# Sparse attention: the second parts of queries and keys stacked into the scores' contraction, the causal mask as a product, and two steps moved later

## The chip, the cores and the metric

The kernel runs on one core of a Trainium2 chip. The metric is the device time of one execution in microseconds; the median of the runs is compared, less is better. The core's engines run side by side, each through its own instructions in order: TensorE (PE in the profile; its weight loads, PEld, overlap its products), VectorE (DVE), ScalarE (ACT), GpSimd (POOL), and SyncE (SP), which here only issues transfers. TensorE writes its results to PSUM, eight banks of 512 fp32 values in each of 128 partitions.

## The reference

Two networks of two layers each run one after the other on 256 tokens of width 1024. Ten stages: feed-forward, S5, feed-forward, feed-forward, convolution, feed-forward, retention, PEER (experts), sparse attention (`nsa`), PEER. The change is in `nsa` alone. Cut to what matters (one batch, 256 tokens, 16 heads of 64 in 4 groups that share keys and values):

```python
kv = (xs @ w_kv)          # three branches, each with keys and values of 4 groups x 64
# branch 0, compressed: blocks of 32 tokens every 16, through a small MLP -> 15 keys and values
hid = gelu(einsum('cbgnf,cfh->cbgnh', blocks, cmp_w1) + cmp_b1); comp = einsum(..., hid, cmp_w2)
q = (h @ w_in)[..., :1024].reshape(...) * 64 ** -0.5;  gate = sigmoid((h @ w_in)[..., 1024:])
o_cmp = softmax(q @ k_cmp, blocks that have ended) @ v_cmp
o_slc = softmax(q @ k_slc, chosen blocks, causal)  @ v_slc
o_win = softmax(q @ k_win, last tokens, causal)    @ v_win
out = gate0 * o_cmp + gate1 * o_slc + gate2 * o_win;  return out @ w_o
```

With 256 tokens every block is chosen and the window covers all, so the second and third branch are plain causal attention over up to 256 keys, each with its own keys and values.

## The kernel before

Large matrix products run as three fp32r products each (`mm3`, lines L281 to L283): both factors are split into a first part (`h`, rounded by a ScalarE copy) and a second part (`l`, what is left, a VectorE subtraction), and hh, hl and lh are summed in PSUM. Weights come as 1 MB units (`wload`), and are split into `wh` (L264) and `wl` (L265). `lin_b` multiplies 256 features (two halves of 128) by all 256 tokens into one PSUM bank; its 48 products have 256 columns. `tile_T` transposes rows of x and writes the split, transposed input (`xTh`, `xTl`); `apply_pending` makes the rows of x themselves (the scale and shift of the layer norm that the stage before left open, L1244 and L1245, two row tiles in halves: eight VectorE operations), which only the residual sum at the end of `nsa` reads.

`nsa` runs in this order. The values `V`; the branch-0 keys and values into `kv2` (two copies of the tokens, the second shifted by one); the keys of branches 1 and 2 into `kT` (`lin_b` for each branch, L1441 and L1442 copy it out of PSUM): fp32, with partitions 0 to 63 holding a group's keys beside zeros and partitions 64 to 127 zeros beside the same keys, so that one product serves two heads that are stacked in the contraction of 128. Then `apply_pending`, the compression (32 input tiles `nsfl`, L1461, times `cmp_w1`, L1463), four query products (`query`, L1475: one ScalarE copy out of PSUM each), the gates.

The attention loop goes over 16 pairs of heads: 8 pairs for query tile 0 (128 queries, n = 128 keys), then 8 for query tile 1 (n = 256). `softmax(i)` computes a pair's scores and weights, `turn(i)` transposes the weights (L1587) and copies them out (half by ScalarE, L1594, half by VectorE, L1592), `attend(i)` multiplies them by the values (L1606). `softmax` runs two pairs ahead of `turn`. The compressed branch (`coarse_softmax`, `coarse_out`) stands in front of the loop and in its first passes; part of the output projection is issued near the end. The scores of a pair, before:

```python
for b in range(2):
    sp = self.mm()                                    # one of two PSUM buffers
    nc.tensor.matmul(sp[...], lhsT=qT[:, g, fb, tile], rhs=kT[:, b, g, :, :n], ...)      # L1565
    v.tensor_tensor(sm[:, b, :, :n], sp[...], mask[...], ALU.add)                        # L1568
v.tensor_reduce(nm, sm[:, :, :, :n], AX.X, ALU.max, negate=True)                         # L1571
for r in range(2):
    for b in range(2):
        nc.scalar.activation(sm[:, b, r, :n], sm[:, b, r, :n], AF.Exp, bias=nm..., accum_out=den...)  # L1574
```

PSUM tiles come from three sets: `acc` (4), `mm` (2) and `tr` (2); a set's next tile waits until the one in its place has been read. `hlp` holds one split transposed input (two tiles of 8 KB a partition), so each `new_T` waits for the last reader of the one before. The order within an engine is not the program's: a planner places each instruction, at build time, where its engine has nothing of higher rank ready, rank being the place in the program; an instruction can so run long before its neighbours. Copies by two engines out of one PSUM bank are put one behind the other at build time.

Of the kernel before, what the change touches and what calls it, by code (L numbers as in the profile page):

```python
# [10 lines left out]
F32 = mybir.dt.float32  # L11
F32R = mybir.dt.float32r
# [183 lines left out]
class Net:  # L196
# [1196 lines left out]
    def nsa(self):  # L1393
# [5 lines left out]
        with ExitStack() as cx:  # L1399
# [14 lines left out]
            mask, cmask = cload("ns_mask", [P, 2, S]), cload("ns_cmask", [P, 2, 2, 16])  # L1414
            pe, b1, w2 = cload("cmp_pe", [P, 2, 16]), cload("cmp_b1", [P, 2, 2]), cload("cmp_w2", [P, 2, 2, 64])
            wg = cload("ns_g", [P, NDC, 48], kp)

# [5 lines left out]
            kv2 = kp.tile([P, 2, 4, S], F32, name="ns_kv2")  # L1423
            for c in range(2):
                ps = self.mm()
                self.lin_b(xh, xl, self.I["ns_kc"][c], ps)
                for g in range(4):
                    q = slice(64 * (g % 2), 64 * (g % 2) + 64)
                    o = g // 2 * S
                    nc.scalar.activation(kv2[0:64, c, g, :], ps[q, o:o + S], AF.Copy)  # L1430
                    v.tensor_copy(kv2[64:128, c, g, 0:S - 1], ps[q, o + 1:o + S])
            kT = np_.tile([P, 2, 4, 2, S], F32, name="ns_kT")
            nc.gpsimd.memset(kT[0:64, :, :, 1, :], 0.0)
            nc.gpsimd.memset(kT[64:128, :, :, 0, :], 0.0)
            for b in range(2):
                ps = self.mm()
                self.lin_b(xh, xl, self.I["ns_k"][b], ps)
                for g in range(4):
                    q = slice(64 * (g % 2), 64 * (g % 2) + 64)
                    o = g // 2 * S  # L1440
                    nc.scalar.activation(kT[0:64, b, g, 0, :], ps[q, o:o + S], AF.Copy)  # L1441
                    v.tensor_copy(kT[64:128, b, g, 1, :], ps[q, o:o + S])  # L1442

            self.apply_pending()
# [4 lines left out]
            kcT = np_.tile([P, 4, 2, 16], F32, name="ns_kcT")  # L1449
            nc.gpsimd.memset(kcT, 0.0)  # L1450
# [3 lines left out]
            for c in range(2):  # L1454
                hp = [self.acc() for _ in range(2)]
                for u in range(2):
                    w1 = self.wload(self.I["cmp_w1"][c, u])
                    for j in range(8):
                        lc = u * 8 + j
                        fl = kp.tile([P, 4, 15], F32, tag="nsfl", bufs=4, name=self.nm("nsfl"))  # L1460
                        v.tensor_scalar(fl, kv2[:, c, :, 2 * lc:2 * lc + 225:16], pe[:, c, lc:lc + 1], None, ALU.add)  # L1461
# [3 lines left out]
                if c == 0:  # L1465
                    self.tile_T((hh, hl), src[1], 1, G, B)
# [3 lines left out]
            qT = np_.tile([P, 4, 2, S], F32, name="ns_qT")  # L1470

            def query(g):
                ps = self.mm()
                self.lin_b(hh, hl, self.I["ns_q"][g], ps)
                nc.scalar.activation(qT[:, g].rearrange("p f t -> p (f t)"), ps, AF.Copy, scale=0.125)  # L1475

            query(0)
            for c in range(2):
# [7 lines left out]
                if c == 0:  # L1486
                    for half in range(2):
                        nc.scalar.activation(kcT[64 * half:64 * half + 64, :, half, :15],
                                             cp[:64, :P].rearrange("p (g n) -> p g n", g=4)[:, :, :15], AF.Copy)
# [3 lines left out]
            query(1)  # L1493
            wgh, wgl = kp.tile([P, NDC, 48], F32R, name="ns_wgh"), kp.tile([P, NDC, 48], F32R, name="ns_wgl")
# [17 lines left out]
            def coarse_softmax(qt):  # L1512
                cs = self.tr()
                for p in range(8):
                    nc.tensor.matmul(cs[:, p * 32:p * 32 + 32], lhsT=qT[:, p // 2, p % 2, qt * P:qt * P + P],
                                     rhs=kcT[:, p // 2].rearrange("p r n -> p (r n)"), start=True, stop=True)
                sc = nw.tile([P, 16, 16], F32, tag="nssc", name=self.nm("nssc"))
                sh = [P, 16, 16]
                v.tensor_tensor(sc, cs[:, :S].rearrange("p (h n) -> p h n", h=16),
                                cmask[:, 0, qt, :].unsqueeze(1).to_broadcast(sh), ALU.add)  # L1520
# [35 lines left out]

            def softmax(i):
# [401 lines left out]
```

## Time and profile before

| | |
|---|---|
| median of 3 runs | 3199.25 us (3197.71 to 3201.43) |
| profiled execution | 3200.87 us, span 3199.1 us |
| mean granted TensorE clock | 0.989 |
| busy share: PE, PEld, DVE, ACT, POOL | 98%, 88%, 78%, 49%, 3% |
| sparse attention, first value product to last attend product | 2165.5 to 2322.4 us |

A busy share is a mean over stages with different limits; a cost in one stage is read from the stretch in which it lies. A profile row gives start, duration, engine, line and operation, out<-in, and behind it in brackets the idle time of the engine before it and what ended that. An fp32 product appears as two records, an fp32r product or a transpose as one. PE durations contain the pipeline's tail, so the price of one of many products is the distance from start to start.

### The profile page before, as it was taken

What the parts mean: (1) busy time and instruction counts of PE and PEld (TensorE: products, weight loads), DVE (VectorE), ACT (ScalarE), POOL (GpSimd) and SP (SyncE); (2) the same over time, 40 slices, a digit from 0 to 9 for tenths busy, and PEclk for the clock granted to TensorE, in tenths of its full rate; (3) what the DMA queues carried; (4) which work ended last, traced back from release to release, by engine and by line L of the source; (5) the groups of instructions that cost most, each with busy time, mean ns of one, the idle gap of its engine ahead of it and who ended that gap; (6) DMA issues with size and microseconds to landing.
All of it is one profiled execution on the core that took longest, in us unless ns stands there. A gap on an engine that the chain in (4) does not pass through costs nothing. (4 is left out here: it accounts for less than half of the span.)

```text
span 3199.1 us, 52281 instructions
## 1 busy us (share of the span) xinstructions
PE 3120.6 (98%) x20484; PEld 2829.5 (88%) x20484; DVE 2508.9 (78%) x4935; ACT 1567.3 (49%) x2350; POOL 105.0 (3%) x172
## 2 busy tenths in 40 slices
PE   8998999999999999999999999999999999999998
PEld 7888899898889888899999998888789999999887
DVE  8877867876986786899976666886789997666787
ACT  5556544446454443545654444335554665444432
POOL 1320000000000000000000000001000000000000
PEclk9999999999999999999999999999999999999999
DMA  5665767674266664445776666665044677566674
GB/s 212 209 230 184 290 228 278 242 287 146 89 242 244 251 250 169 168 153 200 231 255 214 215 215 212 228 226 194 32 159 160 206 235 258 201 215 215 211 239 163
DMA packets 174968, 668.36 MB, mean 209 GB/s; under 512 B 20705, under 2 KB 95233, under 8 KB 101762
## 3 DMA queue, kind: packets, MB, share of 16 engines
q1 hardware_dynamic: 150304, 606.05, 54.0%
q10 hardware_dynamic: 21826, 49.54, 4.1%
q0 software_dynamic: 2592, 9.44, 0.9%
q8 instruction: 161, 2.64, 0.3%
q14 instruction: 85, 0.70, 0.1%
HBM read 619.88 MB, written 45.11 MB: 208 GB/s over the span
## 5 line engine op out<-in xcount | busy, mean ns | idle before, releaser
L264 ACT ACTIVATE wh<-raw 128x1024 fp32r<-128x1024 f32 x948 | 998.5, 1059 | 1199.0 <-PE mm L282 617.6
L265 DVE TENSOR_TENSOR wl<-raw,wh 128x1024 fp32r<-128x1024 f32 x948 | 1150.1, 1221 | 403.9 <-ACT wh L264 392.9
L281 PE MATMUL mm<-xTh,wh 128*128 128x256 f32 x4032 | 1152.5, 286 | 4.5 <-ACT pg L1835 1.7
L283 PE MATMUL mm<-xTh,wl 128*128 128x256 f32 x4032 | 1142.5, 284 | 2.7 <-DVE wl L265 2.7
L282 PE MATMUL mm<-xTl,wh 128*128 128x256 f32 x4032 | 1144.5, 284 | 0.3 <-DVE xTl L355 0.3
L281 PEld LDWEIGHTS mm<-xTh,wh 128*128 128x128 f32 x4032 | 773.5, 192 | 15.7 <-ACT pg L1835 3.2
L282 PEld LDWEIGHTS mm<-xTl,wh 128*128 128x128 f32 x4032 | 773.6, 192 | 8.0 <-issue 0.7
L283 PEld LDWEIGHTS mm<-xTh,wl 128*128 128x128 f32 x4032 | 773.1, 192 | 4.7 <-DVE wl L265 4.4
L283 PE MATMUL acc<-wh,pal 128*128 128x512 f32 x1024 | 403.8, 394 | 0.0
L282 PE MATMUL acc<-wl,pah 128*128 128x512 f32 x1024 | 403.4, 394 | 0.0
L281 PE MATMUL acc<-wh,pah 128*128 128x512 f32 x1024 | 402.9, 393 | 0.0
L283 PEld LDWEIGHTS acc<-wh,pal 128*128 128x128 f32 x1024 | 192.6, 188 | 44.3
L281 PEld LDWEIGHTS acc<-wh,pah 128*128 128x128 f32 x1024 | 193.6, 189 | 39.3
L282 PEld LDWEIGHTS acc<-wl,pah 128*128 128x128 f32 x1024 | 192.7, 188 | 40.1
L1788 ACT ACTIVATE pwb<-tr 128x512 f32<-128x512 f32 x128 | 130.8, 1088 | 24.5 <-PE tr L1785 20.6
L281 PE MATMUL acc<-wh,gh 128*128 128x512 f32 x352 | 141.3, 402 | 0.0
L282 PE MATMUL acc<-wl,gh 128*128 128x512 f32 x352 | 139.8, 397 | 0.0
L283 PE MATMUL acc<-wh,gl 128*128 128x512 f32 x352 | 138.5, 399 | 0.3 <-DVE gl L405 0.3
L1781 DVE TENSOR_SCALAR poh<-pe_iota,pi,pwT 128x128 f32<-128x128 f32 x512 | 136.7, 338 | 0.0
L1849 DVE CAST pah<-pa 128x256 fp32r<-128x256 f32 x256 | 74.7, 293 | 69.6 <-PE acc L282 69.6
L1850 DVE TENSOR_TENSOR pal<-pa,pah 128x256 fp32r<-128x256 f32 x256 | 108.3, 424 | 25.3 <-DVE pah L1849 0.9
L1785 PE MATMUL tr<-poh,poh 128*128 128x128 f32 x1024 | 125.2, 275 | 1.6 <-ACT pwb L1788 1.6
(480 smaller groups left out, 3517.7 us busy)
## 6 DMA issues: line engine op xcount, KB each, us to landing
raw<-in_w SPq DMA_DIRECT2D x132, 1024.0 KB, 4.9
raw<-in_pe_u SPq DMA_DIRECT2D x128, 1024.0 KB, 4.8
raw<-in_pe_v SPq DMA_DIRECT2D x128, 1024.0 KB, 4.8
adaraw<-in_ada_w SPq DMA_DIRECT2D x48, 1024.0 KB, 6.9
pe_wscr<-pwb ACTq DMA_DIRECT2D x32, 1024.0 KB, 8.5
pwr<-pe_wscr SPq DMA_DIRECT2D x30, 1024.0 KB, 6.9
raw<-in_ret_vg SPq DMA_DIRECT2D x16, 1024.0 KB, 4.8
raw<-in_pe_wq SPq DMA_DIRECT2D x16, 1024.0 KB, 4.8
```

What stands on the lines that cost most here:

```text
L264: nc.scalar.activation(h, raw[:, sl], AF.Copy)
L265: nc.vector.tensor_sub(l, raw[:, sl], h.bitcast(F32))
L281: mm(out, lhsT=ah, rhs=bh, start=start, stop=False)
L282: mm(out, lhsT=ah, rhs=bl, start=False, stop=False)
L283: mm(out, lhsT=al, rhs=bh, start=False, stop=stop)
L1781: v.tensor_scalar(oh1[:, j, :], iota[:, :NK], i1[:, t:t + 1], wT[:, t:t + 1], ALU.is_equal, ALU.mult)
L1785: nc.tensor.matmul(ps[:, j * P:j * P + P], lhsT=oh2[:, t4 * 4 + j, :], rhs=oh1[:, t4 * 4 + j, :], start=True, stop=True)
L1788: nc.scalar.activation(wb[:, :, o:o + 4].rearrange("p i t -> p t i"), ps.rearrange("p (t i) -> p t i", t=4), AF.Copy)
L1849: v.tensor_copy(ah, a)
L1850: v.tensor_sub(al, a, ah.bitcast(F32))
```

## The change

Scores: the query tile keeps first parts and second parts of one head stacked in the contraction (64 + 64), and the keys' first parts and second parts lie in two tiles, `kT[0]` and `kT[1]`, each twice (both halves of the partitions). A product with `kT[0]` gives (qh + ql)·kh, one with `kT[1]` (qh + ql)·kl, both fp32r. One PSUM buffer now holds one head and both branches. The causal mask is added by a product of the identity (`one`) with the mask (`low`, twice side by side) over the last 128 keys of each branch. Maximum and exponentials read PSUM; there is no mask add and no copy of the scores in SBUF. The coarse scores take stacked queries too, 16 products of 32 columns per query tile, and one more add.

Order and storage: of the keys' second parts those of branch 1 are made at once, those of branch 2 after the compression's sums of its first half; `apply_pending` moves from ahead of the compression to behind `query(1)`; `softmax(0)` is written ahead of `coarse_softmax(0)`. `kv2` lies in the attention's output tiles, two of the three weight buffers in `hlp`.

```diff
-            mask, cmask = cload("ns_mask", [P, 2, S]), cload("ns_cmask", [P, 2, 2, 16])
+            cmask = cload("ns_cmask", [P, 2, 2, 16])
+            mask = np_.tile([P, P], F32, name="ns_mask")
+            nc.scalar.dma_start(out=mask, in_=self.I["ns_mask"][:, 0, :P])
...
-            kv2 = kp.tile([P, 2, 4, S], F32, name="ns_kv2")
+            kv2 = [o.rearrange("p h d -> p (h d)").rearrange("p (g t) -> p g t", g=4) for o in o_sb]
...
-            kT = np_.tile([P, 2, 4, 2, S], F32, name="ns_kT")
-            nc.gpsimd.memset(kT[0:64, :, :, 1, :], 0.0)
-            nc.gpsimd.memset(kT[64:128, :, :, 0, :], 0.0)
+            halves = [slice(0, 64), slice(64, 128)]
+            kT = [np_.tile([P, 4, 2, S], F32R, name="ns_kT" + i) for i in "hl"]
+            rest = []
+
+            def key_rest():
+                for three in sum(rest, []):
+                    v.tensor_sub(*three)
+                rest.clear()
+
             for b in range(2):
                 ps = self.mm()
                 self.lin_b(xh, xl, self.I["ns_k"][b], ps)
-                for g in range(4):
-                    q = slice(64 * (g % 2), 64 * (g % 2) + 64)
-                    o = g // 2 * S
-                    nc.scalar.activation(kT[0:64, b, g, 0, :], ps[q, o:o + S], AF.Copy)
-                    v.tensor_copy(kT[64:128, b, g, 1, :], ps[q, o:o + S])
-
-            self.apply_pending()
+                for r, q in enumerate(halves):
+                    src_, (h, l) = ps[q].rearrange("p (f t) -> p f t", f=2), (t[:, r::2, b, :] for t in kT)
+                    for d in (q, halves[1 - r]):
+                        nc.scalar.activation(h[d], src_, AF.Copy)
+                    rest.append([(l[d], src_, h[q].bitcast(F32)) for d in (q, halves[1 - r])])
+                if b == 0:
+                    key_rest()
+
+            one = np_.tile([P, P], F32R, name="ns_one")
+            nc.scalar.activation(one, self.ident, AF.Copy)
+            low = np_.tile([P, 2, P], F32R, name="ns_low")
+            for b in range(2):
+                nc.scalar.activation(low[:, b, :], mask, AF.Copy)
+
...
                 if c == 0:
+                    key_rest()
                     self.tile_T((hh, hl), src[1], 1, G, B)
...
-            qT = np_.tile([P, 4, 2, S], F32, name="ns_qT")
+            qT = np_.tile([P, 4, 2, 2, S], F32R, name="ns_qT")
...
-                nc.scalar.activation(qT[:, g].rearrange("p f t -> p (f t)"), ps, AF.Copy, scale=0.125)
+                for r, q in enumerate(halves):
+                    h, l = (qT[d, g, r].rearrange("p f t -> p (f t)") for d in (q, halves[1 - r]))
+                    nc.scalar.activation(h, ps[q], AF.Copy, scale=0.125)
+                    v.scalar_tensor_tensor(l, ps[q], 0.125, h.bitcast(F32), ALU.mult, ALU.subtract)
...
             query(1)
+            self.apply_pending()
...
-                for p in range(8):
-                    nc.tensor.matmul(cs[:, p * 32:p * 32 + 32], lhsT=qT[:, p // 2, p % 2, qt * P:qt * P + P],
-                                     rhs=kcT[:, p // 2].rearrange("p r n -> p (r n)"), start=True, stop=True)
+                for h in range(16):
+                    nc.tensor.matmul(cs[:, h * 32:h * 32 + 32], lhsT=qT[:, h // 4, h % 2, h % 4 // 2, qt * P:qt * P + P],
+                                     rhs=kcT[:, h // 4].rearrange("p i n -> p (i n)"), start=True, stop=True)
...
+            rooms = [t.bitcast(F32).rearrange("p d t -> p (d t)")[:, :4 * S] for t in self.new_T()]
+            rooms.append(nw.tile([P, 4 * S], F32, tag="nssm", bufs=1, name=self.nm("nssm")))
+            rooms = [t.rearrange("p (b r k) -> p b r k", b=2, r=2) for t in rooms]
...
-                sm = nw.tile([P, 2, 2, S], F32, tag="nssm", bufs=3, name=self.nm("nssm"))
-                for b in range(2):
-                    sp = self.mm()
-                    nc.tensor.matmul(sp[:, :2 * n].rearrange("p (r k) -> p r k", r=2),
-                                     lhsT=qT[:, g, fb, qt * P:qt * P + P],
-                                     rhs=kT[:, b, g, :, :n], start=True, stop=True)
-                    v.tensor_tensor(sm[:, b, :, :n], sp[:, :2 * n].rearrange("p (r k) -> p r k", r=2),
-                                    mask[:, qt, :n].unsqueeze(1).to_broadcast([P, 2, n]), ALU.add)
+                sm = rooms[i % 3]
                 nm = nw.tile([P, 2, 2], F32, tag="nsnm", bufs=3, name=self.nm("nsnm"))
-                v.tensor_reduce(nm, sm[:, :, :, :n], AX.X, ALU.max, negate=True)
                 for r in range(2):
+                    sp = self.mm()[:, :2 * n].rearrange("p (b k) -> p b k", b=2)
+                    q = qT[:, g, r, fb, qt * P:qt * P + P]
+                    nc.tensor.matmul(sp, lhsT=q, rhs=kT[0][:, g, :, :n], start=True, stop=False)
+                    nc.tensor.matmul(sp[:, :, n - P:], lhsT=one, rhs=low, start=False, stop=False)
+                    nc.tensor.matmul(sp, lhsT=q, rhs=kT[1][:, g, :, :n], start=False, stop=True)
+                    v.tensor_reduce(nm[:, r, :], sp, AX.X, ALU.max, negate=True)
                     for b in range(2):
-                        nc.scalar.activation(sm[:, b, r, :n], sm[:, b, r, :n], AF.Exp, bias=nm[:, b, r:r + 1],
+                        nc.scalar.activation(sm[:, b, r, :n], sp[:, b, :], AF.Exp, bias=nm[:, r, b:b + 1],
                                              accum_out=den[:, qt, 1 + b, h + r:h + r + 1])
...
+            softmax(0)
             coarse_softmax(0)
-            softmax(0)
             softmax(1)
```

## Rows read from the trace of the kernel before

**Rows 1.** The page's first part: busy us (share of span) and instructions by engine.
```profile
PE 3120.6 (98%) x20484; PEld 2829.5 (88%) x20484; DVE 2508.9 (78%) x4935; ACT 1567.3 (49%) x2350; POOL 105.0 (3%) x172
```

**Rows 2.** Windows: stretch, length, busy us (x instructions) by engine, PEclk, DMA share, GB/s.
```profile
2165.50:2181.10 15.60, 14.92 (x63) 11.62 (x64) 11.89 (x26) 6.34 (x13) 6.12 (x8) 0.89 0.42 130
2181.10:2222.00 40.90, 40.41 (x341) 39.55 (x340) 26.48 (x65) 18.37 (x40) 0.00 (x0) 1.00 0.49 181
2222.00:2247.90 25.90, 25.90 (x218) 25.71 (x216) 13.54 (x13) 15.69 (x21) 0.00 (x0) 1.00 0.67 244
2247.90:2258.10 10.20, 8.45 (x55) 6.81 (x53) 7.71 (x20) 5.97 (x20) 0.00 (x0) 1.00 0.28 104
2258.10:2280.90 22.80, 21.40 (x135) 17.38 (x135) 20.53 (x46) 14.81 (x62) 0.00 (x0) 1.00 0.00 1
2280.90:2322.40 41.50, 40.09 (x260) 31.66 (x259) 31.72 (x50) 21.93 (x74) 0.00 (x0) 1.00 0.00 1
```

**Rows 3.** Timeline of PE in the loop: start, us, line and operation.
```profile
2263.17 1.03 PE L1565 MATMUL mm<-ns_kT,ns_qT 128*128 128x256 f32 x4
2264.03 0.55 PE L1606 MATMUL acc<-ns_V,nspT 128*128 128x64 f32 x4
2264.43 0.39 PE L1587 MATMUL tr<-c_ident,nssm 128*128 128x128 f32 x2
...
2276.66 1.02 PE L1565 MATMUL mm<-ns_kT,ns_qT 128*128 128x512 f32 x2
2277.52 0.27 PE L1587 MATMUL tr<-c_ident,nssm 128*128 128x128 f32 x1
```

**Rows 4.** Groups by line and form, 2281 to 2323 us: busy us, mean ns | idle before.
```profile
L1574 ACT ACTIVATE nssm<-nssm,nsnm 128x256 f32<-128x256 f32 x31 | 15.3, 496 | 1.1 <-DVE nsnm L1571 1.0
...
L1568 DVE TENSOR_TENSOR nssm<-mm,ns_ns_mask 128x512 f32<-128x512 f32 x14 | 9.4, 683 | 1.6 <-PE mm L1565 1.5
L1571 DVE TENSOR_REDUCE nsnm<-nssm 128x4 f32<-128x1024 f32 x7 | 8.4, 1203 | 0.1
...
L1594 ACT ACTIVATE nspT<-tr 128x512 f32<-128x512 f32 x8 | 4.8, 597 | 9.9 <-PE tr L1587 9.7
```

**Rows 5.** The same, 2249 to 2281 us.
```profile
L1574 ACT ACTIVATE nssm<-nssm,nsnm 128x128 f32<-128x128 f32 x32 | 12.4, 389 | 4.9 <-DVE nsnm L1571 4.9
...
L1568 DVE TENSOR_TENSOR nssm<-mm,ns_ns_mask 128x256 f32<-128x256 f32 x16 | 6.4, 414 | 1.5 <-PE mm L1565 1.3
...
L1571 DVE TENSOR_REDUCE nsnm<-nssm 128x4 f32<-128x512 f32 x8 | 5.4, 678 | 0.1
```

**Rows 6.** Waits of PE's weight loads, 2247.9 to 2258.2 us: total, times, longest.
```profile
PEld mm L1565 <- DVE nssm L1568: 2.4, 3, 1.3
```

**Rows 7.** Timeline of PE at the last query and the first coarse scores.
```profile
2246.92 0.28 PE L281 MATMUL mm<-xTh,wh 128*128 128x256 f32 x1
...
2247.04 0.28 PE L282 MATMUL mm<-xTl,wh 128*128 128x256 f32 x1
...
2248.00 1.42 PE L1515 MATMUL tr<-ns_kcT,ns_qT 128*128 128x32 f32 x12
```

**Rows 8.** Timeline of PE in the output projection.
```profile
2316.09 0.39 PE L281 MATMUL acc<-wh,oTh 128*128 128x512 f32 x1
2316.32 0.40 PE L282 MATMUL acc<-wl,oTh 128*128 128x512 f32 x1
```

**Rows 9.** Groups by line and form, 2182 to 2222 us.
```profile
L1463 PEld LDWEIGHTS acc<-nsfl,raw 128*128 128x128 f32 x128 | 14.7, 192 | 0.7 <-DVE nsfl L1461 0.7
...
L1442 DVE COPY ns_kT<-mm 64x256 f32<-64x256 f32 x8 | 3.4, 423 | 3.8 <-ACT ns_kT L1441 3.7
...
L1441 ACT ACTIVATE ns_kT<-mm 64x256 f32<-64x256 f32 x8 | 3.0, 377 | 6.9 <-PE mm L283 4.9 <-DVE ns_kT L1442 1.9
```

**Rows 10.** Timeline of DVE as the stage begins.
```profile
2168.61 0.69 DVE L1244 TENSOR_TENSOR x<-z,rowbc 128x512 f32<-128x512 f32 x1 [1.07 <-DMA rowbc<-in_ln_r]
...
2177.94 0.55 DVE L1496 TENSOR_TENSOR ns_wgl<-ns_ns_g,ns_wgh 128x384 fp32r<-128x384 f32 x1
```

More of the change, by code (lines that the diff above doesn't have):

```diff
@@ L1429, in nsa @@
                     o = g // 2 * S
-                    nc.scalar.activation(kv2[0:64, c, g, :], ps[q, o:o + S], AF.Copy)
-                    v.tensor_copy(kv2[64:128, c, g, 0:S - 1], ps[q, o + 1:o + S])
-            kT = np_.tile([P, 2, 4, 2, S], F32, name="ns_kT")
-            nc.gpsimd.memset(kT[0:64, :, :, 1, :], 0.0)
-            nc.gpsimd.memset(kT[64:128, :, :, 0, :], 0.0)
+                    nc.scalar.activation(kv2[c][0:64, g, :], ps[q, o:o + S], AF.Copy)
+                    v.tensor_copy(kv2[c][64:128, g, 0:S - 1], ps[q, o + 1:o + S])
+            halves = [slice(0, 64), slice(64, 128)]
[5 more added lines that the diff above has]
+                rest.clear()
             for b in range(2):
@@ L1448, in nsa @@
             nc.gpsimd.memset(hid, 0.0)
-            kcT = np_.tile([P, 4, 2, 16], F32, name="ns_kcT")
-            nc.gpsimd.memset(kcT, 0.0)
+            kcT = np_.tile([P, 4, 2, 16], F32R, name="ns_kcT")
+            nc.gpsimd.memset(kcT.bitcast(F32), 0.0)
             vc = np_.tile([P, 4, 64], F32, name="ns_vc")
@@ L1460, in nsa @@
                         fl = kp.tile([P, 4, 15], F32, tag="nsfl", bufs=4, name=self.nm("nsfl"))
-                        v.tensor_scalar(fl, kv2[:, c, :, 2 * lc:2 * lc + 225:16], pe[:, c, lc:lc + 1], None, ALU.add)
+                        v.tensor_scalar(fl, kv2[c][:, :, 2 * lc:2 * lc + 225:16], pe[:, c, lc:lc + 1], None, ALU.add)
                         for hb in range(2):
@@ L1486, in nsa @@
                 if c == 0:
-                    for half in range(2):
-                        nc.scalar.activation(kcT[64 * half:64 * half + 64, :, half, :15],
-                                             cp[:64, :P].rearrange("p (g n) -> p g n", g=4)[:, :, :15], AF.Copy)
+                    cpv = cp[:64, :P].rearrange("p (g n) -> p g n", g=4)[:, :, :15]
+                    for q in halves:
+                        nc.scalar.activation(kcT[q, :, 0, :15], cpv, AF.Copy)
+                    for q in halves:
+                        v.tensor_sub(kcT[q, :, 1, :15], cpv, kcT[:64, :, 0, :15].bitcast(F32))
                 else:
@@ L1513, in coarse_softmax @@
                 cs = self.tr()
-                for p in range(8):
-                    nc.tensor.matmul(cs[:, p * 32:p * 32 + 32], lhsT=qT[:, p // 2, p % 2, qt * P:qt * P + P],
-                                     rhs=kcT[:, p // 2].rearrange("p r n -> p (r n)"), start=True, stop=True)
+                for h in range(16):
+                    nc.tensor.matmul(cs[:, h * 32:h * 32 + 32], lhsT=qT[:, h // 4, h % 2, h % 4 // 2, qt * P:qt * P + P],
+                                     rhs=kcT[:, h // 4].rearrange("p i n -> p (i n)"), start=True, stop=True)
+                cs = cs.rearrange("p (h i n) -> p h i n", h=16, i=2)
                 sc = nw.tile([P, 16, 16], F32, tag="nssc", name=self.nm("nssc"))
                 sh = [P, 16, 16]
-                v.tensor_tensor(sc, cs[:, :S].rearrange("p (h n) -> p h n", h=16),
-                                cmask[:, 0, qt, :].unsqueeze(1).to_broadcast(sh), ALU.add)
+                v.tensor_tensor(sc, cs[:, :, 0, :], cmask[:, 0, qt, :].unsqueeze(1).to_broadcast(sh), ALU.add)
+                v.tensor_add(sc, sc, cs[:, :, 1, :])
                 mx = nw.tile([P, 16], F32, tag="nscm", name=self.nm("nscm"))
```

## The prediction

> **What bounds the kernel now.** I read the page first, for the engine that is never free: TensorE is busy for 98% of the span [rows 1], so what counts is what the change takes from TensorE's queue or adds to it, and the waits in it. Then I cut the attention stage into stretches [rows 2]. From 2181.1 to 2247.9 (values, keys, compression, queries) TensorE is busy all but half a microsecond, while VectorE is busy 26.5 of 40.9 us and then 13.5 of 25.9, and ScalarE 18.4 and 15.7: work added to those two here has room. From 2247.9 the scores begin. Length less PE busy time gives TensorE's idle time there: 1.75 us in the opening, 1.40 in the loop's first half (query tile 0), 1.41 in its second half (query tile 1), 4.6 in all. VectorE is busy 20.5 of 22.8 us in the first half: the one stretch in which it is nearly the bound too. Last I read the rows of one pair [rows 3 to 5], for the price of each operation, and the waits of the opening [rows 6].
>
> **The scores' products.** A pair of heads needs two fp32 products before; each stands in the trace as two records. With 2n = 256 columns, four records take from 2263.17 to 2264.03, 0.86 us a pair; with 512 columns two take 2276.66 to 2277.52, so four take 1.72 [rows 3]. After, each head of the pair takes a product with the keys' first parts, one of 256 columns with the mask, and one with the second parts, all fp32r. The trace has that type in the projections: 512 columns follow each other by 0.23 us (2316.09 to 2316.32), 256 columns by 0.12 (2246.92 to 2247.04) [rows 7, 8]. Query tile 1: 2 × (0.23 + 0.12 + 0.23) = 1.16 us, 0.56 less, × 8 pairs = **-4.5**. Query tile 0: 6 × 0.12 = 0.72, 0.14 less, × 8 = **-1.1**.
>
> **The coarse scores.** Before 8 fp32 products of 32 columns for each query tile, two records each; 12 records take 1.42 us, 0.12 each [rows 7]. After there are 16 fp32r products of 32 columns. No row has that type so narrow. Upper bound 0.12, the price of 256 columns; lower bound 0.06, half of it, though nothing in these rows goes below 0.1. I take 0.12, since 32 and 256 columns cost the same in these rows: 32 × 0.12 against 32 × 0.12, **0**, bounds -1.9 and 0. VectorE gets one more add per tile, 0.41, beside idle time.
>
> **VectorE and ScalarE in the loop.** The mask adds go: 16 of 0.41 and 16 of 0.68 [rows 4, 5], 17.4 us of VectorE. The maximum, one reduce of 0.68 (1.20 for 1024 elements) from SBUF, becomes two from PSUM. No row has a reduce that reads PSUM; the add that reads PSUM takes 0.683 for 512 elements and the reduce from SBUF 0.678 [rows 4, 5], so I take 0.41 for 256 elements and 0.68 for 512: +0.14 and +0.16 a pair, +2.4 us in all. VectorE falls by 15 us of the 52 that it is busy in the loop. The exponentials keep their number and size and read PSUM; ScalarE's copies out of PSUM take 0.60 for 512 elements, the exponential from SBUF 0.50 for 256 [rows 4], so I leave 0.49 from one start to the next, 0.39 for 128 columns [rows 5].
>
> **What the buffers do.** A score buffer ("mm", two of them) was free once the mask add had read it. Now it is held until two exponentials have. Query tile 1: first head 0.58 for products, 0.27 to VectorE, 0.68, 0.05, 0.98 of exponentials: 2.56 us after the pair began. The second head's exponentials queue behind on ScalarE and end at 3.54; its buffer is wanted 0.58 into the next pair, so a period of 3.06 will do, or 3.66 with ScalarE's 0.60 copy of transposed weights between. TensorE's own period is 1.16 + 24 records (8 transposes, 16 for the values) of 0.10 [rows 3] = 3.6: the buffer is hidden, if barely. Query tile 0: 0.36 + 0.27 + 0.41 + 0.05 + 0.77 = 1.86, second head 2.63, period 2.63 + 0.1 - 0.36 = 2.37, or 2.8 with the copy of half the width (0.4, an estimate from the 0.60); TensorE's own is 0.72 + 12 × 0.10 = 1.9. Here the buffer is late, unless other products (coarse, transposes of a pair ahead, of which three buffers of weights allow two) fill in.
>
> **The waits in the loop.** In the opening TensorE's weight loads wait 2.4 us for the mask add [rows 6]; that wait has no instruction left to wait for. In its place: the last query is split by two copies and two subtractions, which take turns as the keys' copies do in the trace, 2 × (0.60 + 0.68) = 2.6 us where one copy of that width took 0.60 [rows 4]. Score 1 needs the buffer that this frees, and coarse heads 12 to 15 need its result. What can be issued meanwhile: coarse heads 0 to 11 (1.4) and score 0 (0.36). So 0.8 us idle, then about as much for the exponentials of pair 0: I take **-1.0**, between -1.75 (none left) and +1.5 (nothing fills in). In the first half, 1.40 idle with VectorE 90% busy; it loses about a third of its work, so its waits go, against the late buffer, up to 7 × 0.45 = 3.2. I take **-0.9**, between -1.4 and +3.2. In the second half **0**, down to -1.4.
>
> **Keys, queries, rows of x.** Keys: eight copies of 0.38 on ScalarE and eight of 0.42 on VectorE [rows 9] become eight of 0.60 and eight of 0.68, +1.8 and +2.1 us. Of the eight subtractions four follow their product at once, four stand behind the compression's first sums. VectorE is idle 14 us of that stretch; what is late if the cover fails is the compression's input tiles, for which TensorE's loads already wait 0.7 us [rows 9]. Cost 0, bounds -0.7 and +1.5. Queries: one copy each becomes two copies and two subtractions: ScalarE +2.4 us over four queries, VectorE +5.4; with their 15.7 and 13.5 of 25.9 us both stay under 20. Cost 0 while TensorE is supplied. ScalarE also makes one identity and two mask copies, and POOL's two fills of the key tile go; neither holds anything here. The mask's load is a quarter of its size on the same queue: 0.
>
> The eight operations on the rows of x come later in the program. In the trace they do not stand where the program has them: they fill VectorE's idle moments from 2168.61 on, and the subtraction for the gate weights, written much later still, comes right behind them at 2177.94 [rows 10]. So the engine order takes whatever is ready, and I expect these eight at the same place: **0**. Were they to leave, the first one's wait of 1.07 us for its DMA would leave the queue with them, and the normalisation queued behind it would come earlier: at best the 0.68 us that TensorE idles in that stretch [rows 2] plus some of its 1.07, -1.0 to -1.5. Were they to land among the queries, VectorE would have 13.5 + 5.4 + 5.4 = 24.3 of 25.9 us.
>
> **The sum.** -4.5 - 1.1 - 1.0 - 0.9 = -7.5 us. The profiled execution took 3200.87 us around a span of 3199.1; it becomes 3193.4. That execution is 1.6 above the median of 3199.25; against the median, 3191.75. Behind the attention TensorE is the bound again [rows 1], so what is won there is kept.
>
> **The rivals.** *The buffers eat half.* The late buffer in the first half costs its whole 3.2 us and no other wait there goes: -5.6 + 3.2 - 1.0 = -3.4, 3195.85. For: two buffers, one queue for all exponentials. Against: 1.2 of TensorE's 1.9 us in such a pair are not scores and can be issued meanwhile.
>
> *Slower: both buffers wait for the whole pair.* If the engine order puts a pair's four exponentials and the copy of transposed weights in front of the next pair's first product, the period is a chain: query tile 1, 1.16 + 0.27 + 0.68 + 4 × 0.49 + 0.6 + 0.15 = 4.8 against some 4.3 now (41.5 less some 7 for the projection's 24 products of 0.23 and 12 transposes, over 8); query tile 0, 0.72 + 0.27 + 0.41 + 4 × 0.39 + 0.4 + 0.15 = 3.5 against some 2.3 (0.86 + 1.2, and the idle 1.40 over 7 pairs). That is +4 and +9.6, less the 1.0 of the opening and some 3 that other products fill: +10, 3209. It decides from where the chain passes 3.6 and 1.9 us, TensorE's own periods. Against it: pairs run two ahead, and today ScalarE stands idle at the end of each pair. The Trainium skill ("VectorE: DVE Perf Modes", Rules for kernel authors) would lean this way: work on a matmul's output should first be copied to SBUF if many operations follow. The kernel before does that, with the mask add as the copy; the change reads PSUM three times instead. By that rule the time would be this rival's; no row here has such a reader, and the rows' price of a PSUM operand shows no surcharge [rows 4, 5].
>
> *The rows of x do leave the start:* -7.5 - 1.2, 3190.6. *They, or the subtractions, crowd the queries:* VectorE nearly full, TensorE short by some 2.5 us, 3194.25; the change then does half of what it says.
>
> **Chances.** Faster or slower is beyond 6.4 us, 0.2%, about what a measurement of this kernel can tell. The forecast 0.52 (its own range 3189 to 3194, so 0.43 of it beyond 6.4 us and 0.09 within), rows of x leave 0.12 (faster), buffers eat half 0.20 and crowded queries 0.04 (within), whole-pair chain 0.12 (slower). Faster 0.55, within 0.33, slower 0.12. Range 3187 to 3201: it holds all but the chain and a small rest below, where the narrow coarse products cost half and all waits go.
>
> **What would show it.** Right: no VectorE adds between score and maximum; score records at 0.23 and 0.12; the stretch from the last query's product to the last attend product 74.5 us before, 67 after; VectorE well under 80% there; the eight operations on x still in 2168 to 2178. Wrong: score loads that wait for exponentials for more than 3 us in all (buffers), a first half as long as before, or TensorE gaps between 2182 and 2248. A fall of the granted clock in the stage, now 1.00 from 2181 to 2322 [rows 2], would also break the sum.

## The result and the profile after

The changed kernel takes 3215.32 us (median of 6, 3211.72 to 3217.05), the kernel before 3198.48 beside it (median of 6, 3195.2 to 3201.43): a ratio of 1.0051, 95% interval 1.004 to 1.0062. The forecast was 3191.75. The profiled span is 3212.8 us, 13.7 more than before. (The medians lie 16.8 apart: the profiled execution of the kernel before was 2.4 above its median, that of the changed kernel 0.7 below.)

The page's first part, as in [rows 1]: all engines do about what they did.

```profile
PE 3130.8 (97%) x20516; PEld 2846.2 (89%) x20516; DVE 2504.5 (78%) x4931; ACT 1570.3 (49%) x2357; POOL 101.2 (3%) x170
```

Windows of the stage, columns as in [rows 2]: compression and queries, opening, rest of query tile 0, query tile 1.

```profile
2206.00:2259.50 53.50, 51.21 (x356) 50.31 (x355) 31.06 (x61) 25.73 (x42) 0.00 (x0) 0.81 0.47 177
2259.50:2270.00 10.50, 7.95 (x39) 6.61 (x38) 8.09 (x16) 7.65 (x26) 0.00 (x0) 0.66 0.29 101
2270.00:2293.50 23.50, 22.74 (x150) 20.40 (x148) 14.67 (x40) 11.40 (x51) 0.00 (x0) 0.86 0.00 1
2293.50:2336.00 42.50, 40.41 (x292) 36.26 (x291) 25.99 (x46) 22.56 (x81) 0.00 (x0) 1.00 0.00 1
```

The column to read is PEclk. Before, it was 1.00 in every stretch from 2181.1 on [rows 2]; now it is 0.81, 0.66 and 0.86 in three of the four stretches. Length times (1 - PEclk) is the most that the lower clock can cost: 10.2 us in the first, 3.6 + 3.3 in the next two. The length counts waits too; with TensorE's busy time in its place, in steps of half a microsecond, it is 9.9 and 2.9 + 3.2. In windows of 2 us (TensorE alone) one sees two falls to 0.50, that is 1.2 GHz, the first 0.9 us into a wait of TensorE, the second right behind one:

```profile
2214.00:2216.00 2.00, 0.38 (x3) 0.76 0.44 70
2216.00:2218.00 2.00, 2.00 (x10) 0.50 1.00 422
...
2234.00:2236.00 2.00, 2.00 (x13) 0.62 0.99 410
```
```profile
2260.00:2262.00 2.00, 1.57 (x14) 1.00 0.26 33
2262.00:2264.00 2.00, 1.24 (x6) 0.71 0.92 360
2264.00:2266.00 2.00, 2.00 (x7) 0.50 0.31 131
...
2276.00:2278.00 2.00, 2.00 (x14) 0.88 0.00 0
```

What TensorE waited for around the first fall (0.67 us up to 2212.15, then 1.62 up to 2215.77) is in the list of waits, and VectorE's timeline says why: the second branch's subtractions (L1442) stand in its queue ahead of the compression's input tiles (nsfl, L1478).

```profile
PE acc L1480 <- DVE nsfl L1478: 2.3, 2, 1.6
PE mm L281 <- DVE ns_o L1435: 0.6, 1, 0.6
```
```profile
2209.73 0.27 DVE L1478 TENSOR_SCALAR nsfl<-ns_o,ns_cmp_pe 128x60 f32<-128x60 f32 x1 [0.17 <-PE acc L1480]
2210.03 0.68 DVE L1442 TENSOR_TENSOR ns_kTl<-mm,ns_kTh 64x512 fp32r<-64x512 f32 x1
2210.64 1.28 DVE L344 TENSOR_TENSOR xTl<-hT,xTh 128x512 fp32r<-128x512 f32 x2
2211.84 0.80 DVE L1478 TENSOR_SCALAR nsfl<-ns_o,ns_cmp_pe 128x60 f32<-128x60 f32 x4
2212.67 2.10 DVE L1442 TENSOR_TENSOR ns_kTl<-mm,ns_kTh 64x512 fp32r<-64x512 f32 x3
...
2215.45 0.44 DVE L1478 TENSOR_SCALAR nsfl<-ns_o,ns_cmp_pe 128x60 f32<-128x60 f32 x2
```

Ahead of the second, TensorE's timeline at the opening: 13 coarse products, then a wait for the last query's split, behind which the clock falls; the waits for exponentials (0.39 and 0.94 us) come after the fall. From 2262.76 on the 256-column products follow each other by 0.21 or more instead of 0.12.

```profile
2259.88 1.72 PE L1539 MATMUL tr<-ns_kcT,ns_qT 128*128 128x32 f32 x13
2262.76 0.48 PE L1597 MATMUL mm<-ns_kTh,ns_qT 128*128 128x256 f32 x1 [1.16 <-DVE ns_qT L1496]
2263.04 0.41 PE L1598 MATMUL mm<-ns_low,ns_one 128*128 128x256 f32 x1
2263.25 0.41 PE L1599 MATMUL mm<-ns_kTl,ns_qT 128*128 128x256 f32 x1
...
2268.37 0.58 PE L1597 MATMUL mm<-ns_kTh,ns_qT 128*128 128x256 f32 x1 [0.94 <-ACT xTl L1602]
```

Four marks of TensorE's timeline cut the stage for all that follows: the first compression product, the first product of the scores (fine or coarse), the first score of 512 columns, the end of the last attend product. Their distances, us, from one profiled execution of each kernel:

| kernel | compression, queries | query tile 0 | query tile 1 | all | time, median | ratio to before, 95% |
|---|---|---|---|---|---|---|
| before | 43.61 | 27.37 | 46.89 | 117.87 | 3198.48 | |
| after | 53.51 | 33.99 | 42.37 | 129.87 | 3215.32 | 1.004 to 1.0062 |
| e1 subtractions behind | 42.54 | 34.06 | 42.37 | 118.97 | 3202.97 | 1.0001 to 1.0021 |
| e2 before, with a burst | 54.24 | 27.39 | 46.89 | 128.52 | 3210.35 | 1.002 to 1.0043 |
| e3 rows of x early | 53.22 | 33.83 | 42.37 | 129.42 | 3215.74 | 1.0034 to 1.0067 |
| e4 more input tiles | 41.78 | 34.42 | 42.35 | 118.55 | 3200.25 | 0.9996 to 1.0015 |
| e7 e4, coarse first | 41.77 | 31.65 | 42.33 | 115.75 | 3198.38 | 0.999 to 1.0009 |
| e9 e4, copies first | 41.78 | 32.44 | 42.36 | 116.58 | 3201.82 | 1.0001 to 1.002 |
| e8 e4, narrow repeats | 41.76 | 35.43 | 41.41 | 118.60 | 3201.41 | 0.9997 to 1.0016 |
| e12 e4, wide repeats | 41.78 | 33.78 | 42.36 | 117.92 | 3202.72 | 1.0001 to 1.002 |
| e16 e9, table early | 41.78 | 32.27 | 42.43 | 116.48 | 3200.81 | 0.9995 to 1.0014 |
| e15 e16, wide repeats | 41.77 | 31.58 | 42.39 | 115.74 | 3200.34 | 0.9999 to 1.0019 |
| e18 e16, fewer repeats | 41.77 | 30.68 | 42.42 | 114.87 | 3198.2 | 0.999 to 1.0008 |

So the 13.7 us are +9.9 in compression and queries, +6.6 in query tile 0, -4.5 in query tile 1, +0.1 behind, and +1.6 ahead of the first mark. Of these 1.6, 0.6 is the new wait for ns_o above, and the rest is no loss: eight transposes of the input (L329, 0.12 us each), which the kernel before issues among the compression's products (2206.56 to 2208.02), stand ahead of them in every changed kernel. The first column is so about 1.0 us too kind to the changed kernels: like for like, the first loss is some 10.9. From the first value product to the last attend product it is 156.73 us before and 170.45 after. The parts outside vary: over all these traces the first compression product stands at 2201.2 to 2207.2, and 875.4 to 880.7 us follow the last attend product. Differences of the stage below some 3 us therefore show in the table's stretches and not in the times.

### The profile page after: what moved, and what is told of

Read it like the earlier page. It is cut to its first block, busy times and chain, and to the rows that moved or that the text cites. A ratio compares the mean times of both kernels' runs of the same rounds, so it can differ in the third digit from the quotient of the medians.

```text
span 3212.8 us, 52370 instructions
## 1 busy us (share of the span) xinstructions
PE 3130.8 (97%) x20516; PEld 2846.2 (89%) x20516; DVE 2504.5 (78%) x4931; ACT 1570.3 (49%) x2357; POOL 101.2 (3%) x170
```

## The experiments

**The first fall.** Theory A: the burst of subtractions holds up the input tiles, TensorE idles, and the half clock behind that is most of the loss. Rivals: the split work itself, or a clock that falls there in any case.

*e1* moves the second branch's subtractions behind the last input tile:

```
-                    key_rest()
...
+            with self.tc.issue_after(last_fl.ins):
+                key_rest()
```


> The changed kernel with one edit: the second branch's four key subtractions (0.68 us each) are ordered behind the last input tile of the compression in VectorE's queue, so that TensorE no longer waits for input tiles in the second half of the compression. Theory A (the burst of subtractions holds the compression's input tiles up, TensorE idles 0.7 and 1.6 us, and its granted clock then stands at 0.50 for some 20 us): the granted clock stays at 1.00 from 2206 on to the last query's product, that product ends about 11 to 12 us earlier, and the time falls from 3215 to 3203 to 3205. Rival B (the time is lost to the doubled copies and subtractions of keys and queries themselves, which TensorE's products of the queries then wait for): the waits stay about where the queries are, and the time stays at 3212 to 3216. Rival C (the half clock comes whatever VectorE does there, from the stage itself): the window of 0.50 moves but stays as long, time 3211 to 3216.

Measured 3202.97, the faster edge of what theory A forecast. PEclk is 1.00 in every window from 2206 to 2248, and no wait for input tiles is in the list. Theory A; B and C fall.

*e2* puts such a burst into the kernel before, between the last input tile of the compression's first half and the first of its second half, which is ordered behind it (that line is left out here):

```
+                    for k in range(4):
+                        with self.tc.issue_after(last_fl.ins if k == 0 else burst.ins):
+                            burst = v.tensor_sub(o_sb[0][0:64] ..., kv2[0:64, 0, 0:2, :], kv2[0:64, 1, 0:2, :])
```


> The kernel before with one addition: four VectorE subtractions of 64x512 whose result nobody reads, put between the last input tile of the compression's first half and the first of its second half (2.1 to 2.8 us of VectorE work). No part of the change is in it. Theory A: TensorE waits some 1.5 to 3 us for input tiles there, the granted clock falls to 0.50 for 10 to 20 us behind it, and the time grows by 8 to 13 us over the kernel before (3207 to 3212). Rival B (the burst is not what costs): it grows by no more than the wait, 0 to 3 us (3198 to 3201).

Measured 3210.35; the stretch grows by 10.6 us, the two others not at all. TensorE has two waits there, 1.27 us up to 2214.02 for which the profile names no releaser and 1.69 us up to 2216.80 for an input tile; the clock falls 0.7 us into the first. In windows of TensorE:

```profile
2212.00:2214.00 2.00, 0.75 (x7) 0.86 1.08 328
2214.00:2216.00 2.00, 1.09 (x4) 0.50 0.72 307
...
2232.00:2234.00 2.00, 2.00 (x12) 0.52 0.74 197
2234.00:2236.00 2.00, 2.00 (x19) 1.00 1.04 426
```

Four subtractions of 0.67 that touch no data of the change give its first loss: at 0.50 from 2214 to 2232 alone the lower clock costs 8 to 9 us (busy time or length), nearly three times the waits.

*e4* leaves the burst and lets VectorE run ahead of it:

```
-  tag="nsfl", bufs=4
+  tag="nsfl", bufs=16
```


> The changed kernel with 16 buffers instead of 4 for the compression's input tiles, so that VectorE can make them well ahead of TensorE and the burst of subtractions finds them made. Theory A: TensorE's waits for input tiles go, the granted clock stays at 1.00 there, and the time falls by 9 to 12 us, to 3203 to 3206. Rival B (doubled split work of keys and queries): no change, 3212 to 3216. Rival D (the subtractions must run somewhere and take the queries' place if they don't take the input tiles'): the gain is 3 to 6 us only, with new waits of TensorE for the splits of the queries.

Measured 3200.25, 2.8 less than the forecast of 3203 to 3206; the stretch takes 41.78 us, 1.8 below the kernel before, of which 1.0 is the transposes that stand ahead of the mark. Theory A again, by another remedy; D falls, no new wait for the splits of the queries comes up in that stretch. The stretch in e1 and in e4, TensorE alone:

```profile
2202.64:2245.18 42.54, 42.54 (x356) 1.00 0.62 223
2203.76:2245.54 41.78, 41.78 (x357) 1.00 0.63 227
```

*e3* applies the rows of x at their old place:

```
+            self.apply_pending()
...
-            self.apply_pending()
```


> The changed kernel with the rows of x applied at their old place (ahead of the compression) again. As the rows are ready at about 2168 to 2178 in both traces and the order of VectorE's queue comes out the same, every theory here expects no change: 3213 to 3217. A rival by which the rows' late place delays something (their DMAs or their subtractions colliding with the queries) would give 2 to 5 us back.

Measured 3215.74: that part of the change does nothing.

**The second fall.** All that follows stands on e4. *e5* makes the first pair's scores and exponentials ahead of the last query's product:

```
+            softmax(0)
             query(3)
...
-            softmax(0)
-            coarse_softmax(0)
             softmax(1)
+            coarse_softmax(0)
```


> The changed kernel with 16 input tiles in the compression (as in the run before it) and, on top, the scores and exponentials of the first head pair ahead of the last query's product, which they do not need; what is then behind that product is the second pair's scores (no need of the last query either), the coarse scores and the first pair's transposes. Theory A (the second loss is at the opening: TensorE waits 1.16, 0.47, 0.66 and 0.94 us for the last query's split and the first exponentials, and its granted clock then stands at 0.50 for some 14 us, which costs about 7): the waits shrink to under 1 us in all, the clock stays at 1.00 between 2248 and 2264, and the time falls by 5 to 9 us, to 3191 to 3196, below the kernel before. Rival E (the clock falls at the start of the scores whatever the waits, as the small products themselves let it fall): a window of 0.50 stays, and the time stays at 3198 to 3202.

Measured 3206.8 (ratio 1.0015 to 1.0035), worse than e4. The waits moved and grew: the engine order brought coarse products in with the first pair, where they wait for the third query's split, and the last query waits for a buffer ("mm") that this split still holds: TensorE waits 2.8 us in all for the splits at the coarse products and 1.3 us at the last query. This tells nothing between A and E, but it shows that a query's buffer is held until its second subtraction.

*e7* has the coarse scores first again (`coarse_softmax(0)` ahead of `softmax(0)`, as before).

> The changed kernel with 16 input tiles in the compression and, on top, the coarse scores' softmax ahead of the first pair's again, as in the kernel before; that undoes the last part of the change. TensorE has then the same work before the last query's split is there (13 of 16 coarse products, 1.6 us), but the first exponentials come later, and the score of the first pair can no longer cover the wait. Theory A: the waits at the opening and the window at 0.50 stay or grow: 3199 to 3204. Rival F (that exchange is itself the loss): the opening is as in the kernel before, the clock stays at 1.00, and the time is 3192 to 3196.

Measured 3198.38, query tile 0 2.8 us shorter than in e4; the clock still falls (0.50 from 2254 to 2262), a wait of 1.1 us for the split stands ahead of it. Neither forecast fits whole: F's clock did not stay up, and A had the waits stay or grow and the time at 3199 to 3204. The exchange cost 2.8 us of query tile 0 on e4 alone, and is not the whole; on e9 and on e16 (below) undoing it gained nothing.

*e9* makes both copies of a query ahead of both subtractions.

```
+                for q, (h, l) in zip(halves, hls):
+                    nc.scalar.activation(h, ps[q], AF.Copy, scale=0.125)
+                for q, (h, l) in zip(halves, hls):
+                    v.scalar_tensor_tensor(l, ps[q], 0.125, h.bitcast(F32), ALU.mult, ALU.subtract)
```


> The changed kernel with 16 input tiles in the compression and, on top, both ScalarE copies of a query ahead of both VectorE subtractions, instead of copy, subtraction, copy, subtraction. The last query's split should end some 0.6 us earlier. Theory A by its waits: the 1.16 us becomes about 0.5, the table load starts 0.6 earlier, and the clock falls later or for less; gain 1 to 5 us (3195 to 3199). Rival E (the waits do not decide): no change, 3199 to 3202.

Query tile 0 is 2.0 us shorter, as A had it; the 1.16 us wait became 0.41 and 0.53. The time, 3201.82, does not show it; it lies where rival E had it. Another run (e6) was to load the Exp table early, but its exponential depended on nothing, was put ahead of the sigmoid, and the load of 1.28 us stayed in the opening (3201.11): no verdict. e7 and e9 together (e14, 3199.21) took 32.58 us for query tile 0, no less than one alone.

*e8* fills the waits with repeated products that change no value, 12 coarse ones and 20 of the scores:

```
-                for h in range(16):
+                for h in [*range(12 if qt == 0 else 0), *range(16)]:
...
+                    for _ in range(2 if i < 5 else 0):
+                        nc.tensor.matmul(sp, lhsT=q, rhs=kT[0][:, g, :, :n], start=True, stop=True)
```


> The changed kernel with 16 input tiles in the compression and, on top, products at the opening that are done again and change no value: 12 of the first coarse products twice (1.4 us in the wait for the last query's split) and the first product of each score of the first five pairs three times instead of once (20 products of 0.12 us, in the waits for the exponentials). No wait is taken away and VectorE and ScalarE do the same; TensorE only idles less. Theory A, sharpened by the three runs before (waits of other lengths and places at the opening, the same half clock behind all of them): it is TensorE's idling there, the scores being now too short for it, that brings the granted clock down. Then the clock stays at 1.00 between 2246 and 2270 and the time falls by 5 to 7 us, to 3193 to 3196, below the kernel before. Rival E (the stage's waits themselves are the loss, the clock adds nothing to them, as VectorE and ScalarE bound the opening): 3199 to 3204.

Theory A in this form falls. TensorE is busier than before in the opening, and the clock falls all the same. Windows of e8, and of the kernel before at the same place:

```profile
2248.00:2250.00 2.00, 2.00 (x20) 1.00 0.51 119
2250.00:2252.00 2.00, 1.85 (x14) 0.85 0.96 406
2252.00:2254.00 2.00, 1.85 (x9) 0.50 0.00 0
```
```profile
2250.00:2252.00 2.00, 1.92 (x9) 1.00 0.81 283
2252.00:2254.00 2.00, 1.12 (x5) 1.00 0.52 217
2254.00:2256.00 2.00, 1.75 (x13) 1.00 0.01 4
...
2260.00:2262.00 2.00, 1.32 (x12) 1.00 0.00 0
```

The kernel before idles 0.96 of the first 4 us and 2.5 of the 12 at 1.00, with 256-column fp32 products between; e8 idles 0.15 of 4 us, with 25 products of 32 columns behind each other, and falls. The busy time that a profile shows does not tell the two apart. The time, 3201.41, lies where rival E had it. (The coarse repeats alone, e10, 3201.14, fell too; so did e8 with e9 and e6 in it, e11, 3201.36.)

*e12* repeats only the 256-column products, ten times in the first score and twice in each other of five pairs.

> The changed kernel with 16 input tiles in the compression; on top, the first score's first product (256 columns) is done eleven times and that of the other scores of the first five pairs three times, each over the one before, so that no value changes; the coarse products are done once. 10 products of 0.12 us lie ahead of the wait for the last query's split and cover it, 18 more lie in the waits for exponentials. Theory G (it is not the idle time in the trace but how little the short products of the opening make TensorE do that brings the clock down; the 32-column repeats of the earlier run filled the time and did not hold the clock): the clock stays at 1.00 from 2246 to 2270, the first half of the scores is some 6 us shorter, and the time is 3192 to 3196. If the clock falls again by 2252: 3199 to 3203.

Between the two in the trace: the clock held until a wait of 1.73 us for exponentials, then 0.50 from 2258 to 2264, some 7 us at half rate in place of 14. The time, 3202.72, is that of a fall. (e13, with the copies and the coarse scores first, 512-column repeats ahead of the coarse scores and two repeats in each score of five pairs, 3203.81: a wait of 2.28 us, then as e12.)

*e16* and *e15* load the table behind the sigmoid, with an exponential that reads its output, and make both copies first; e15 has the wide repeats besides.

```
             nc.scalar.activation(gT, gp[:48, :S], AF.Sigmoid)
+            nc.scalar.activation(warm, gT[:, :1], AF.Exp)
```


> The same without any repeated product: 16 input tiles, both copies first, the Exp table behind the sigmoid. Shorter waits alone: the first query tile's scores 30 to 32 us (32.44 with the table in the opening), the half clock still there; 3196 to 3200. If the table load was what decided: 1.00 throughout, 3191 to 3195.

> The changed kernel with 16 input tiles, both copies of a query first, the Exp table loaded behind the sigmoid (a one-column exponential of the sigmoid's output that nobody reads), and wide repeats: the first score's first product eleven times, that of the other scores of the first five pairs four times. The first exponentials come about 1.3 us earlier and TensorE has products of 256 columns for most of the time that it waited. Theory A/G: no wait over 0.5 us is left in the opening, the granted clock stays at 1.00 from 2246 to 2280, the first query tile's scores take 25 to 28 us instead of 33 to 34, and the time is 3191 to 3196. If a window of 0.50 comes all the same, neither idling nor the products' width is what I think it is: 3199 to 3203.

The two differ in the repeats alone. Windows of e16, then of e15:

```profile
2250.00:2252.00 2.00, 1.58 (x12) 1.00 0.81 225
2252.00:2254.00 2.00, 1.27 (x8) 0.87 0.71 299
2254.00:2256.00 2.00, 1.59 (x7) 0.50 0.00 0
...
2262.00:2264.00 2.00, 2.00 (x6) 0.57 0.03 8
```
```profile
2250.00:2252.00 2.00, 1.82 (x12) 1.00 0.30 127
2252.00:2254.00 2.00, 0.97 (x6) 1.00 0.00 0
2254.00:2256.00 2.00, 1.83 (x15) 1.00 0.00 0
...
2262.00:2264.00 2.00, 2.00 (x19) 1.00 0.00 0
```

e15 does 37 products more (4.4 us at 0.12) and its query tile 0 is 0.7 us shorter, at the full clock throughout, with a wait of 1.0 us left in it. In these profiled executions, e16's waits for the split and the exponentials, none above 0.43 us, did not hold the clock. The forecast of 25 to 28 us for that tile left the repeats' own time out, and the time, 3200.34, missed its 3191 to 3196; it is not apart from e16's 3200.81. (e17, e16 with the coarse scores first: 32.61 us, 3201.2.)

*e18* keeps the repeats for three pairs, 25 products.

> As the run with 16 input tiles, both copies first, the Exp table behind the sigmoid and wide repeats, but with the repeats on the first three pairs alone (25 products). If the clock is held by what lies between 2246 and 2255: 1.00 throughout, the first query tile's scores 30.0 to 30.6 us instead of 31.58, the stage 114.2 to 114.8 us, the time 3196 to 3199, a little below the kernel before. If the repeats on the fourth and fifth pair were needed as well: a window of 0.50 behind 2255, scores of 32 to 34 us, and 3199 to 3202.

The clock stays at 1.00 through query tile 0:

```profile
2246.15:2276.83 30.68, 28.36 (x213) 1.00 0.10 36
```

The stage is 114.87 us, 3.0 below the kernel before between these marks, but 1.2 below it from the first value product on (155.57 against 156.73), since the transposes and the wait for ns_o then count. The time is 3198.2 beside 3198.76, ratio 0.9999 (0.999 to 1.0008). So no version was measurably faster than the kernel before.

That the repeats hold the clock does not rest on single profiles alone. The mean granted clock of every execution is on record: 0.989 to 0.991 in all 11 of e18, 0.986 to 0.991 in the 10 of e16, seven of them below 0.989. But it is a mean over the whole kernel, and so varies in the kernel before as well (0.988 to 0.992 beside e18). Two executions of e16, at 0.990 and 0.991, took 3197.09 and 3195.05: without any repeat some executions lost less of the clock, at the opening or elsewhere, and the profiled one (0.987, 3203.04) is among the slow ones.

## Why the prediction was wrong, point by point

**Keys, queries, rows of x: "Cost 0, bounds -0.7 and +1.5".** This is the step that failed first. The prediction named what would be late ("the compression's input tiles") and took VectorE's 14 idle us in the stretch as cover. An average over 41 us said nothing of 5 us in which three subtractions stand in a row: the waits were 2.3 us in all, beyond the bound. And it priced a wait at its own length. Here it brought some 10 us of lower clock with it: +9.9 between the marks, some 10.9 like for like, instead of 0, shown by e1, e2 and e4 from both sides. The sign set for this step, "TensorE gaps between 2182 and 2248", came. That a fall of the clock "would also break the sum" stood in the prediction as a remark, with neither chance nor price. The new wait of 0.6 for ns_o had no term either. The rows of x were right: they stayed at 2168 to 2178 (the first at 2168.38, ns_wgl at 2177.84), and e3 measures no effect.

**The waits in the loop: -1.0 and -0.9.** Neither came; the stretch from the last query's product to the last attend product, forecast at 67 us, is 76.4. TensorE idles 3.3 us of query tile 0 (34.0 less 30.69 busy) as against 1.75 + 1.40 before [rows 2]. The wait for the last query's split was forecast at 0.8 and is 1.16: a weight split of 1.23 stands ahead of it on VectorE, and the copies and subtractions take turns as the prediction said. The forecast had no term for the table load of 1.28 us ahead of the first exponential (before, it stood at the same place, 2248.81, but ScalarE then waited 2.13 us more for the maximum). Then the clock: 6.1 to 6.9 us of the 34.0. Without it the tile takes 27.1 to 27.9 us, about what it took before, where 24.4 was forecast; that is arithmetic, not a run. What the runs show is less: with the clock held the tile takes 30.68 us (e18) where e16 takes 32.27, with 25 repeats, 3.0 us at 0.12, in it, and it is still 3.3 above the kernel before. So the clock is shown to be part of this second loss, and not that it is all of it. Why it fell at the opening stays open.

**The scores' products: -4.5 and -1.1.** Right: query tile 1 is 4.5 us shorter. The products stand at the forecast steps, 0.23, 0.12 and 0.23 or so:

```profile
2317.58 0.40 PE L1597 MATMUL mm<-ns_kTh,ns_qT 128*128 128x512 f32 x1
2317.82 0.28 PE L1598 MATMUL mm<-ns_low,ns_one 128*128 128x256 f32 x1
2317.93 0.40 PE L1599 MATMUL mm<-ns_kTl,ns_qT 128*128 128x512 f32 x1
2318.17 0.22 PE L1634 MATMUL acc<-ns_V,nspT 128*128 128x64 f32 x1
```

The same 1.1 cannot be read out of query tile 0, where the clock moves. **The coarse scores**, 0: right, 13 products take 1.72 us with the last one's end, 0.12 to 0.13 each.

**VectorE, ScalarE and the buffers.** The prices were right. The maximum from PSUM takes 0.683 us for 512 elements, against 0.678 from SBUF [rows 5], and the exponential from PSUM 0.474 for 256, against 0.496 [rows 4]:

```profile
L1600 DVE TENSOR_REDUCE nsnm<-mm 128x2 f32<-128x512 f32 x16 | 10.5, 683 | 2.1 <-PE mm L1599 2.0
...
L1602 ACT ACTIVATE nssm<-mm,nsnm 128x256 f32<-128x256 f32 x12 | 5.5, 474 | 2.0 <-DVE nsnm L1600 2.0
```

VectorE is busy 25.99 of the last 42.5 us, as against 31.72 of 41.5 [rows 2]; over opening and loop it falls by 11.2 us (59.96 to 48.75), not 15, as the last query's two subtractions and the coarse adds lie there too. The buffers were late: the sign set for "the buffers eat half", score loads that wait more than 3 us for exponentials, came, with 4.5 us from 2259.5 to 2336 (0.2 of it not shown):

```profile
PEld mm L1597 <- ACT xTl L1602: 2.8, 3, 1.2
PEld mm L1597 <- ACT nssm L1602: 1.5, 3, 0.8
```

The products themselves waited 2.7 us, half of it in query tile 0 at the half clock; query tile 1 still gained its whole 4.5. So that rival was there in small, and is not the loss. "The whole-pair chain" did not happen, for query tile 1 would have lost 4 us by it; its 3209 lies nearest to the result all the same: the right side for the wrong reason. The rule of the Trainium skill that was set beside that rival ("VectorE: DVE Perf Modes", Rules for kernel authors) leaves a choice: accept the base rate from PSUM, or copy a matmul's output to SBUF first if many operations follow. The trace shows the first to be right here: these readers took about as long from PSUM as from SBUF, so a copy had nothing to win.

**What stays open:** what a version that holds the clock at the opening in every execution without added products would gain; and why the clock fell in e8, behind 25 narrow products in a row, and not in the kernel before, with more idling.

## What to carry to other kernels

Where TensorE runs at its full clock through a stage, give a new wait in it a price for the clock besides its length, and a wide range: in e2 two waits of 3.0 us in all cost 10.6. The kernel before had one such place, a wait of 2.22 us as the stage begins, and behind it the clock cost 1.7 us (6.00 at 0.72). So its trace showed that a wait can bring the clock down, but not how far:

```profile
2165.53 0.51 PE L281 MATMUL mm<-wh,xTh 128*128 128x512 f32 x1 [2.22 <-ACT xTh L343]
2166.00:2172.00 6.00, 5.87 (x21) 0.72 0.48 158
```

Give moved work on a second engine a place in that engine's queue, instruction by instruction, since idle time averaged over a stretch covers no burst; more buffers for the waiting input are the cheap insurance (e4). And where a change makes the bound engine's products shorter while other engines set the pace, forecast the granted clock there as a term of its own, with both levels priced.

## What the runs showed of the hardware

In e2 the clock fell 0.7 us into a wait of 1.27 us, a wait of 1.69 us followed, and it stood at 0.50 from 2214 to 2232, though TensorE was busy 2.00 of 2.00 us in each window from 2218 on. Behind a wait of 2.22 us in the kernel before, its low stretch cost 1.7 us. A wait of 1.73 us in e12 was followed by a fall, one of 1.0 us in e15 was not. Busy 1.85 of 2 us fell (e8) and 1.12 of 2 did not (before). An Exp after a Sigmoid brings a table load of 1.28 us on ScalarE, at the first exponential. A VectorE reduce (0.683 us for 512 elements against 0.678) and a ScalarE exponential (0.474 for 256 against 0.496) took about as long from PSUM as from SBUF. Executions of one kernel differed in the mean granted clock (e16: 0.986 to 0.991), and those with more of it were the faster ones (3203.53 to 3195.05).
